# Side steps of the expert scoring stage: their place in VectorE's queue, the order of a wide block's products, and gates for sixteen tokens at a time

## Chip, cores, metric

One core of one Trainium2 chip runs the whole program in one launch. The metric is the device time of the program in microseconds, as the median of several executions.

## What is computed

A two-layer decoder on 256 tokens of width 1024. Layer 0 mixes tokens with a sparse attention, layer 1 with a forgetting attention; each is followed by an expert layer, and at the end stands a norm. The change touches the expert layer alone, which runs once in each layer:

```python
def peer_ffn(x, w_q, sub_keys, u, v):
    q = (x @ w_q).reshape(B, S, PEER_HEADS, 2, hq)
    s_half = jnp.einsum('bshpc,hpkc->bshpk', q, sub_keys)
    top_s, top_i = lax.top_k(s_half, PEER_TOPK)          # 16 of 128, two halves, 8 heads
    cand_s = top_s[..., 0, :, None] + top_s[..., 1, None, :]
    best_s, best_pos = lax.top_k(cand_s.reshape(B, S, PEER_HEADS, 256), PEER_TOPK)
    gate = jax.nn.softmax(best_s, axis=-1)
    h = jax.nn.gelu(jnp.einsum('ted,td->te', u[ec], xc))  # the chosen experts of each token
    return jnp.einsum('te,ted->td', gate * h, v[ec])
```

There are 128 x 128 = 16384 experts. The kernel gathers none: it multiplies every token by all of u, weights the result with a gate that is zero for the experts that were not chosen, and multiplies by all of v.

## The kernel before

All products are of split numbers: a weight tile is rounded (`hi`, a cast on ACT, L116) and the rest is kept beside it (`lo`, a subtraction on VectorE, L117), and hi·hi, hi·lo and lo·hi are added up in PSUM. TensorE is named PE below, VectorE DVE, ScalarE ACT, GpSimd POOL, SyncE SP.

The expert layer (`peer`) has three stages. In the first, x is multiplied by w_q in 16 blocks of columns, and each block is scored against its keys. In the second, **u's stage**, 128 blocks of u (128 experts each) are multiplied with all 256 tokens. In the third, v's stage, 128 blocks of v are multiplied with the gated result. This is about u's stage, whose loop over b stands at L1044 to L1049. One turn of it does this:

- `load_split(uT[b])` (L758): SP loads a tile `raw` of 128x1024, ACT casts it to `hi` (L116), DVE subtracts to get `lo` (L117). Each of `raw`, `hi` and `lo` has three buffers, so that the tiles of block b+3 take those of block b.
- The products, into a PSUM tile `h` of which there are two, so that block b+2 takes that of block b. Even blocks run `feat_block` (L774), called f below: for each of 8 chunks three products of 256 columns (L778, L781, L782). Odd blocks run `wide_block` (L1014), called W: for each chunk one product of 512 columns (hi with both halves of x, L1019) and one of 256 (lo, L1020), alternating. A W block leaves two halves in PSUM, which are added: ACT copies one out (`u`, written to a tile `vraw`, L1022), DVE adds the other (L1023). This is called the add below; it frees the PSUM tile.
- `values(b, o)` (L1025): the gelu on ACT (L1031), and for tokens whose gates stand already a product on DVE (L1035).
- Steps of a generator `aux`, until their nominal costs add up to 1.5 us a block: what is left of the top 16 keys (`top_keys`, L812), the best pairs (`best_pairs`, L905), and the gates (`gate_steps`, L983).

`gate_steps` builds the gates of 8 tokens at a time: DVE compares an index table `iota` with the tokens' two chosen rows (L991, L992), multiplies with the gate's two parts (L994, L995), PE multiplies one-hot by one-hot, 16 products of 128 columns in half precision (L1002, L1003), into PSUM tiles `m`, and the result is multiplied into what stands there by DVE (L1009) or copied by ACT (L1011). The one-hots take a 4 KB buffer of the three called `vhl` and a 2 KB one of the four called `vraw`.

Every engine runs its queue in order. The order is set by a scheduler when the program is built: it takes instructions in the program's order, lets those that it holds ready go ahead, and goes by its own costs. So a step can stand in DVE's queue well before the place at which the loop asked for it, among it before the `lo` and the add of a block that PE is about to need.

```python
        for b in range(NB):
            values(b, (wide_block if b % 2 else feat_block)(load_split(uT[b])))
            if b < 2:
                scores(14 + b, qTs[14 + b])
            while spent < 1.5 * (b + 1):
                spent += next(aux, 1e9)
```

Of the kernel before, what the change touches and what calls it, by code (L numbers as in the profile page):

```python
# [8 lines left out]
F32 = mybir.dt.float32  # L9
F32R = mybir.dt.float32r  # L10
F16 = mybir.dt.float16
# [6 lines left out]
P = 128  # L18
S = 256
# [20 lines left out]
def body(ctx, tc, A, out):  # L40
# [14 lines left out]
    iota = const.tile([P, 4, P, 2], F16, name="iota")  # L55
# [52 lines left out]
    def late_consts():  # L108
        V.tensor_copy(identb, ident)
        GP.iota(iota, pattern=[[0, 4], [1, P], [0, 2]], base=0, channel_multiplier=0, allow_small_or_imprecise_dtypes=True)  # L110
        mtmp = t2k(P)
        SP.dma_start(mtmp, A["cmask"])
        V.tensor_copy(maskb, mtmp)

    def split(raw, hi, lo, eng=None):
        ACT.copy(hi, raw)  # L116
        (eng or V).tensor_tensor(lo, raw, hi.bitcast(F32), ALU.subtract)  # L117
# [639 lines left out]

    def load_split(src, eng=None):  # L758

        raw = tl(ustr, "raw", [8, P], bufs=3)  # L760
        SP.dma_start(raw, src)
        hi = tl(ustr, "hi", [8, P], F32R, 3)
        lo = tl(ustr, "lo", [8, P], F32R, 3)
        if eng is None:
            split(raw, hi, lo)
        parts = []
        for hf in range(2):
            cs = slice(4 * hf, 4 * hf + 4)
            if eng is not None:
                split(raw[:, cs], hi[:, cs], lo[:, cs], eng[hf])  # L770
            parts.append((hi[:, cs], lo[:, cs]))
        return parts
# [12 lines left out]
    def peer(li, norm, mark):  # L785
# [27 lines left out]
        def top_keys():  # L813
            for b in range(16):
                for tt in range(2):
                    s1, s2 = sb[b][:, tt], ar(S2 + ((2 * b + tt) % 4) * 128, P)
                    V.max(topf[:, tt, b, 0:8], s1)
                    V.max_index(idx[:, tt, b, 0:8], topf[:, tt, b, 0:8], s1)
                    V.match_replace(s2, topf[:, tt, b, 0:8], s1, FMIN)
                    V.max(topf[:, tt, b, 8:16], s2)  # L820
                    V.max_index(idx[:, tt, b, 8:16], topf[:, tt, b, 8:16], s2)
                    yield 1.4
# [17 lines left out]
        for b in range(16):  # L840
# [11 lines left out]
            while tops + 1.4 <= min(2.8 * len(scored), 2.5 * (b - 2)):  # L852
                tops += next(keyed)
# [52 lines left out]
        def best_pairs():  # L906
# [22 lines left out]
            for hh in range(16):  # L929
# [7 lines left out]
                yield 1.0  # L937
# [24 lines left out]
            for tt in range(2):  # L962
                yield 2.0
# [19 lines left out]
        def gate_steps():  # L983


            for t0 in range(0, S, 8):
                ohb, ol = t4k(2, 4, P, 2, dt=F16), t2k(4, P, 2, dt=F16)
                o2, oh = ohb[:, 0], ohb[:, 1]
                row = lambda i: (hkT[:, i, t0:t0 + 8].rearrange("p (q t) -> p q t", q=4)
                                 .unsqueeze(2).broadcast_to((P, 4, P, 2)))  # L990
                V.tensor_tensor(o2, iota, row(1), ALU.is_equal)  # L991
                V.tensor_tensor(oh, iota, row(0), ALU.is_equal)  # L992
                yield 1.4
                V.tensor_tensor(ol, oh, row(3), ALU.mult)  # L994
                V.tensor_tensor(oh, oh, row(2), ALU.mult)  # L995
                pgs = []
                for q in range(2):
# [7 lines left out]
                yield 1.4  # L1005
                for q in range(2):
# [6 lines left out]
                yield 1.2  # L1013

        def wide_block(parts):
            o = pst("h")
            for c in range(8):
                hi, lo = parts[c // 4]
                PE.matmul(o, hi[:, c % 4], x2[:, c].rearrange("p a t -> p (a t)"), start=c == 0, stop=False)  # L1019
                PE.matmul(o[:, :S], lo[:, c % 4], xh[:, c], start=False, stop=c == 7)  # L1020
# [23 lines left out]
        for b in range(NB):  # L1044
# [3 lines left out]
            while spent < 1.5 * (b + 1):  # L1048
                spent += next(aux, 1e9)  # L1049
# [161 lines left out]
```

## Time and profile before

| what | value |
|---|---|
| median of 3 runs | 1937.56 us (1936.56 to 1938.04) |
| the profiled execution's own time | 1937.12 us |
| its span, first to last instruction | 1935.4 us |
| mean granted clock of PE | 0.997 |
| busy PE, DVE, ACT, POOL | 1900.9, 1435.3, 1030.1, 107.7 us |
| PE waiting to start, where W blocks wait for the add (L1019 for DVE L1023) | 5.2 us, 7 times |
| the same by the weight load, which comes first | 8.3 us, 14 times |

Matmuls are pipelined: a row's duration is longer than the time until the next one starts, so what PE takes for a piece of work is read from start to start, and not as a sum of durations. The same holds, less strongly, for DVE: the next instruction starts about 0.08 us before the one before it ends.

### The profile page before, as it was taken

Reading aid. Unit: us, or ns where it says so; the run is one execution under the profiler, and the core shown is the slowest. Engines: PE = TensorE matmul, PEld = TensorE weight load, DVE = VectorE, ACT = ScalarE, POOL = GpSimd, SP = SyncE. Lnnn points to the kernel's source line nnn. Section 1 sums busy time; section 2 is a strip of 40 time slices with the busy share of each in tenths; the row PEclk is TensorE's granted clock in tenths of the full one; section 3 lists DMA queues with packets and bytes.
Section 4 is the critical chain, followed back from the end, with each engine's and each line's share of the span. In section 5 each row is a group of like instructions: output and inputs, shape, how many; then the busy total and the mean of one; then the engine's idle time right before and its main releaser. Section 6 shows DMA issues by size and latency. Waiting matters only on the chain.

```text
span 1935.4 us, 32159 instructions
## 1 busy us (share of the span) xinstructions
PE 1900.9 (98%) x12107; PEld 1660.8 (86%) x12107; DVE 1435.3 (74%) x3016; ACT 1030.1 (53%) x2038; POOL 107.7 (6%) x76
## 2 busy tenths in 40 slices
PE   8889999999999999999999999999999999999998
PEld 6767989999999888888889799899999988888886
DVE  8687997788899655565676799968889975555555
ACT  4475655555555544454554655555555554444444
POOL 2001700000000000000000061000000000000001
PEclk9999999999999999999999999999999999999999
DMA  6713445545545665567644245554545556555564
GB/s 228 271 39 121 163 164 177 174 164 164 164 164 164 218 206 195 192 213 256 220 156 152 71 164 162 172 182 161 167 161 164 164 178 215 195 195 192 191 205 141
DMA packets 91051, 340.79 MB, mean 176 GB/s; under 512 B 9968, under 2 KB 12432, under 8 KB 85776
## 3 DMA queue, kind: packets, MB, share of 16 engines
q1 hardware_dynamic: 90608, 338.22, 52.9%
q8 instruction: 95, 1.56, 0.3%
q14 instruction: 60, 0.49, 0.1%
q10 hardware_dynamic: 288, 0.52, 0.1%
HBM read 334.48 MB, written 4.19 MB: 175 GB/s over the span
## 4 chain that ended last, share of the span: by engine, by line
PE 88%; DVE 8%; ACT 3%; DMA 1%; issue 1%; POOL 0%; SPq 0%; ACTq 0%; DVEq 0%
PE m L1071 12%; PE m L1070 12%; PE m L1072 12%; PE h L1019 11%; PE h L778 6%; PE h L781 6%; PE h L782 6%; PE h L1020 6%; DVE lo L117 2%; PE m L203 2%; PE m L201 2%; PE m L202 2%; PE m L1002 2%; PE m L1003 2%; PE m L695 1%; PE m L694 1%
## 5 line engine op out<-in xcount | busy, mean ns | idle before, releaser
L117 DVE TENSOR_TENSOR lo<-raw,hi 128x1024 fp32r<-128x1024 f32 x516 | 633.5, 1228 | 375.5 <-ACT hi L116 373.2
L116 ACT CAST hi<-raw 128x1024 fp32r<-128x1024 f32 (+1 forms) x572 | 576.3, 1010 | 504.2 <-PE m L1072 312.5
L1071 PE MATMUL m<-lo,vhl 128*128 128x512 f32 x1024 | 398.6, 389 | 0.0
L1072 PE MATMUL m<-hi,vhl 128*128 128x512 f32 x1024 | 398.4, 389 | 0.0
L1070 PE MATMUL m<-hi,vhl 128*128 128x512 f32 x1024 | 398.3, 389 | 0.0
L1019 PE MATMUL h<-x,hi 128*128 128x512 f32 x1024 | 372.5, 400 | 5.4 <-DVE vraw L1023 5.2
L1020 PE MATMUL h<-x,lo 128*128 128x256 f32 x1024 | 291.7, 285 | 0.0
L778 PE MATMUL h<-x,hi 128*128 128x256 f32 x1024 | 289.3, 283 | 0.9 <-ACT E L1031 0.9
L782 PE MATMUL h<-x,lo 128*128 128x256 f32 x1024 | 289.8, 283 | 0.0
L781 PE MATMUL h<-x,hi 128*128 128x256 f32 x1024 | 289.7, 283 | 0.0
L1019 PEld LDWEIGHTS h<-x,hi 128*128 128x128 f32 x1024 | 192.4, 188 | 46.5 <-DVE vraw L1023 8.3
L1071 PEld LDWEIGHTS m<-lo,vhl 128*128 128x128 f32 x1024 | 192.2, 188 | 40.3 <-DVE lo L117 0.5
L1070 PEld LDWEIGHTS m<-hi,vhl 128*128 128x128 f32 x1024 | 192.1, 188 | 40.1 <-ACT hi L116 0.4
L1072 PEld LDWEIGHTS m<-hi,vhl 128*128 128x128 f32 x1024 | 192.2, 188 | 39.9
L778 PEld LDWEIGHTS h<-x,hi 128*128 128x128 f32 x1024 | 193.1, 189 | 6.6 <-ACT E L1031 1.4
L782 PEld LDWEIGHTS h<-x,lo 128*128 128x128 f32 x1024 | 192.8, 188 | 0.0
L781 PEld LDWEIGHTS h<-x,hi 128*128 128x128 f32 x1024 | 192.8, 188 | 0.0
L1020 PEld LDWEIGHTS h<-x,lo 128*128 128x128 f32 x1024 | 192.6, 188 | 0.0
L117 POOL TENSOR_TENSOR lo<-raw,hi 128x512 fp32r<-128x512 f32 x56 | 78.8, 1426 | 261.8 <-ACT hi L116 261.6
L117 DVE TENSOR_TENSOR E<-arena,E 128x1024 fp32r<-128x1024 f32 (+2 forms) x60 | 67.1, 1140 | 10.8 <-ACT E L116 10.5
L778 PE MATMUL h<-E,hi 128*128 128x256 f32 x240 | 70.3, 293 | 3.0 <-ACT arena L851 3.0
L116 ACT CAST E<-arena 128x1024 fp32r<-128x1024 f32 (+2 forms) x64 | 58.6, 952 | 21.6 <-PE m L694 9.7
(314 smaller groups left out, 2772.8 us busy)
## 6 DMA issues: line engine op xcount, KB each, us to landing
raw<-in_u SPq DMA_DIRECT2D x256, 512.0 KB, 3.5
raw<-in_v SPq DMA_DIRECT2D x256, 512.0 KB, 4.1
arena<-in_w_in SPq DMA_DIRECT2D x16, 1024.0 KB, 5.9
raw<-in_wq SPq DMA_DIRECT2D x32, 512.0 KB, 3.5
arena<-in_w SPq DMA_DIRECT2D x8, 1024.0 KB, 5.0
arena<-in_w_out SPq DMA_DIRECT2D x8, 1024.0 KB, 5.1
hd<-arena SPq DMA_DIRECT2D x3, 1024.0 KB, 3.9
arena<-hd SPq DMA_DIRECT2D x3, 1024.0 KB, 5.6
```

The source lines that it names most:

```text
L116: ACT.copy(hi, raw)
L117: (eng or V).tensor_tensor(lo, raw, hi.bitcast(F32), ALU.subtract)
L201: PE.matmul(o[:, :n], sh[:, cc, tsl], wh[:, c], start=cc == 0, stop=False)
L202: PE.matmul(o[:, :n], sh[:, cc, tsl], wl[:, c], start=False, stop=False)
L778: t = PE.matmul(o[:, :S], hi[:, c % 4], sh[:, c], start=c == 0, stop=False)
L781: PE.matmul(o[:, :S], hi[:, c % 4], sl[:, c], start=False, stop=False)
L782: PE.matmul(o[:, :S], lo[:, c % 4], sh[:, c], start=False, stop=c == 7)
L1019: PE.matmul(o, hi[:, c % 4], x2[:, c].rearrange("p a t -> p (a t)"), start=c == 0, stop=False)
L1020: PE.matmul(o[:, :S], lo[:, c % 4], xh[:, c], start=False, stop=c == 7)
L1070: PE.matmul(acc[tt][nh], gh[:, ts], vh, start=first, stop=False)
L1071: PE.matmul(acc[tt][nh], gh[:, ts], vl, start=False, stop=False)
L1072: PE.matmul(acc[tt][nh], gl[:, ts], vh, start=False, stop=last)
```

## The change

Five edits, all in `peer` and its helpers.

1. `load_split` keeps the `lo` of the last block that was split, and the loop traces its steps under `issue_after` of it: in DVE's queue each step then stands behind that `lo`. This orders the queue when the program is built; no semaphore is added.
2. The nominal costs change: 1.25 in place of 1.4 for a step of the top keys, 1.3 in place of 1.0 for one of the pairs, 0.4 in place of 2.0 ahead of the transposes, and 1.46 us of steps a block in place of 1.5.
3. A wide block does its eight products of 512 columns first, then its eight of 256.
4. Gates are built for 16 tokens at a time: four operations on 2048 elements in place of eight on 1024, 32 products of PE in one piece in place of two pieces of 16, four PSUM tiles `m` (all there are) for one piece. The one-hots take all three `vhl` buffers.
5. The index table has one copy in place of four (256 elements a partition), and is read by a broadcast.

```diff
     def split(raw, hi, lo, eng=None):
         ACT.copy(hi, raw)
-        (eng or V).tensor_tensor(lo, raw, hi.bitcast(F32), ALU.subtract)
+        return (eng or V).tensor_tensor(lo, raw, hi.bitcast(F32), ALU.subtract)
...
         if eng is None:
-            split(raw, hi, lo)
+            split_of["last"] = split(raw, hi, lo).ins
...
-                    yield 1.4
+                    yield 1.25
...
-            while tops + 1.4 <= min(2.8 * len(scored), 2.5 * (b - 2)):
+            while tops + 1.25 <= min(2.5 * len(scored), 2.5 * (b - 2)):
...
-                yield 1.0
+                yield 1.3
...
-                yield 2.0
+                yield 0.4
...
-            for t0 in range(0, S, 8):
-                ohb, ol = t4k(2, 4, P, 2, dt=F16), t2k(4, P, 2, dt=F16)
-                o2, oh = ohb[:, 0], ohb[:, 1]
-                row = lambda i: (hkT[:, i, t0:t0 + 8].rearrange("p (q t) -> p q t", q=4)
-                                 .unsqueeze(2).broadcast_to((P, 4, P, 2)))
-                V.tensor_tensor(o2, iota, row(1), ALU.is_equal)
-                V.tensor_tensor(oh, iota, row(0), ALU.is_equal)
-                yield 1.4
+            for t0 in range(0, S, 16):
+                o2, oh, ol = (t4k(8, P, 2, dt=F16) for _ in range(3))
+                row = lambda i: (hkT[:, i, t0:t0 + 16].rearrange("p (q t) -> p q t", q=8)
+                                 .unsqueeze(2).broadcast_to((P, 8, P, 2)))
+                index = iota.unsqueeze(1).broadcast_to((P, 8, P, 2))
+                V.tensor_tensor(o2, index, row(1), ALU.is_equal)
+                yield 1.2
+                V.tensor_tensor(oh, index, row(0), ALU.is_equal)
+                yield 1.2
                 V.tensor_tensor(ol, oh, row(3), ALU.mult)
+                yield 1.2
                 V.tensor_tensor(oh, oh, row(2), ALU.mult)
                 pgs = []
-                for q in range(2):
+                for q in range(4):
...
-                yield 1.4
-                for q in range(2):
+                yield 1.2
+                for q in range(4):
...
                     done[1] += 4
-                yield 1.2
+                    yield 0.6
 
         def wide_block(parts):
             o = pst("h")
             for c in range(8):
-                hi, lo = parts[c // 4]
-                PE.matmul(o, hi[:, c % 4], x2[:, c].rearrange("p a t -> p (a t)"), start=c == 0, stop=False)
-                PE.matmul(o[:, :S], lo[:, c % 4], xh[:, c], start=False, stop=c == 7)
+                PE.matmul(o, parts[c // 4][0][:, c % 4], x2[:, c].rearrange("p a t -> p (a t)"), start=c == 0, stop=False)
+            for c in range(8):
+                PE.matmul(o[:, :S], parts[c // 4][1][:, c % 4], xh[:, c], start=False, stop=c == 7)
...
-            while spent < 1.5 * (b + 1):
-                spent += next(aux, 1e9)
+            with tc.issue_after(split_of["last"]):
+                while spent < 1.46 * (b + 1):
+                    spent += next(aux, 1e9)
```

Line numbers move by a few: the add is L1027 after the change (L1023 before), the wide products L1022 and L1024 (L1019, L1020), the gate operations on DVE L993, L995, L997, L999, the gate products L1006, L1007.

How the queues change is shown at three places. The first is DVE's queue early in u's stage of layer 0: `lo_360`, `lo_364` and `lo_369` are the splits of blocks 4, 5 and 6, the tile `vraw_357` is written by the add of block 3, L817 to L821 (L819 to L823 with the change) are steps of the top keys, and L924 and L909 the start of the best pairs. Before:

```order
L117 TENSOR_TENSOR lo_364_2853<-raw_362_2850,hi_363_2852 128x1024
L821 MAX_INDEX arena_58<-arena_58 128x8
L819 MATCH_REPLACE arena_58<-arena_58 128x128
L924 TENSOR_TENSOR arena_58<-arena_58 128x16x8
L820 MAX arena_58<-arena_58 128x8
L924 TENSOR_TENSOR arena_58<-arena_58 128x16x5
L821 MAX_INDEX arena_58<-arena_58 128x8
L924 TENSOR_TENSOR arena_58<-arena_58 128x16x16
L909 CAST arena_58<-arena_58 128x512
L117 TENSOR_TENSOR lo_369_2885<-raw_367_2882,hi_368_2884 128x1024
L1023 TENSOR_TENSOR vraw_357_2804<-h_356_2787,vraw_357_2804 128x256
```

and with the change:

```order
L117 TENSOR_TENSOR lo_360_2831<-raw_358_2828,hi_359_2830 128x1024
L822 MAX arena_58<-arena_58 128x8
L819 MAX arena_58<-arena_58 128x8
L823 MAX_INDEX arena_58<-arena_58 128x8
L820 MAX_INDEX arena_58<-arena_58 128x8
L821 MATCH_REPLACE arena_58<-arena_58 128x128
L117 TENSOR_TENSOR lo_364_2868<-raw_362_2865,hi_363_2867 128x1024
L822 MAX arena_58<-arena_58 128x8
L823 MAX_INDEX arena_58<-arena_58 128x8
L117 TENSOR_TENSOR lo_369_2900<-raw_367_2897,hi_368_2899 128x1024
L1027 TENSOR_TENSOR vraw_357_2819<-h_356_2802,vraw_357_2819 128x256
```

The add of block 3 stands behind the split of block 6 in both. Between the splits of blocks 5 and 6 stood eight operations of steps, and now two; over the whole way from the split of block 3 to this add it is 20 in place of 24, and the four that went are the start of the best pairs, which is now asked for behind the split of block 6. Further on, the sixteen steps of the best pairs (L932 to L936 before) stood between the splits of blocks 7 and 14, two or three a block; now they stand between those of blocks 8 and 22, one a block and at two places two.

The second place is PE's queue where gates are built (the tile `m` is the gates' PSUM, `h` that of a block). Before, a piece of 16 gate products stands inside a block, most often behind the ninth product of a W block:

```order
L1020 MATMUL h_664_4921<-x2_59,lo_663_4918 128x256
L1019 MATMUL h_664_4921<-x2_59,hi_662_4917 128x512
L1002 LDWEIGHTS vhl_644_4816
L1002 MATMUL m_652_4852<-vhl_644_4816 128x128
L1003 LDWEIGHTS vhl_644_4816
L1003 MATMUL m_652_4852<-vraw_645_4817,vhl_644_4816 128x128
```

and with the change a piece of 32 stands between two blocks:

```order
L784 MATMUL h_616_4617<-x2_59,lo_615_4614 128x256
L1022 MATMUL h_621_4653<-x2_59,hi_619_4649 128x512 x8
L1024 MATMUL h_621_4653<-x2_59,lo_620_4650 128x256 x8
L1006 LDWEIGHTS vhl_610_4606
L1006 MATMUL m_624_4678<-vhl_611_4607,vhl_610_4606 128x128
L1007 LDWEIGHTS vhl_610_4606
```

Of a layer's 32 pieces before, 31 stood inside a block; of the 16 now, one does (the first, inside block 39), and the last stands behind block 112 (before: inside block 123). The wide products stand in runs of eight.

The third place is DVE's queue at the same stage, with the change: the four operations of one piece (L993, L995, L997, L999), each behind a split of its own or the next.

```order
L117 TENSOR_TENSOR lo_644_4798<-raw_642_4795,hi_643_4797 128x1024
L1027 TENSOR_TENSOR vraw_622_4670<-h_621_4653,vraw_622_4670 128x256
L993 TENSOR_TENSOR vhl_639_4791<-iota_63,hkT_337_2674 128x2048
L1039 TENSOR_TENSOR E_336_2670<-vraw_623_4674,E_336_2670 128x48
L995 TENSOR_TENSOR vhl_640_4792<-iota_63,hkT_337_2674 128x2048
L117 TENSOR_TENSOR lo_649_4834<-raw_647_4831,hi_648_4833 128x1024
L1039 TENSOR_TENSOR E_336_2670<-vraw_632_4746,E_336_2670 128x48
L1013 SCALAR_TENSOR_TENSOR E_336_2670<-m_624_4678,E_336_2670 128x55x4
L1013 SCALAR_TENSOR_TENSOR E_336_2670<-m_625_4687,E_336_2670 128x55x4
L997 TENSOR_TENSOR vhl_641_4793<-vhl_640_4792,hkT_337_2674 128x2048
L1027 TENSOR_TENSOR vraw_637_4778<-h_636_4761,vraw_637_4778 128x256
L117 TENSOR_TENSOR lo_655_4865<-raw_653_4862,hi_654_4864 128x1024
```

The rows are those of blocks 56 to 58: a split of every block, an add of every second, and one or two long steps between.

On POOL the index table is built ahead of everything else in both; with the change a clearing of 64x1024 (L369) stands between the first two of POOL's four splits of the program's first weights. SP's queue of u's loads stands as it was.

## Rows read from the trace of the kernel before

**Rows 1.** The page, part 1: busy time, share of the span, instructions.

```profile
PE 1900.9 (98%) x12107; PEld 1660.8 (86%) x12107; DVE 1435.3 (74%) x3016; ACT 1030.1 (53%) x2038; POOL 107.7 (6%) x76
```

**Rows 2.** PE's timeline, ends of layer 0's u stage: start, duration, instruction, count.

```profile
239.92 0.37 PE L778 MATMUL h<-x,hi 128*128 128x256 f32 x1
...
643.70 0.40 PE L1070 MATMUL m<-hi,vhl 128*128 128x512 f32 x1
```

**Rows 3.** PE's timeline, first product of an f block and of the next block.

```profile
331.75 0.28 PE L778 MATMUL h<-x,hi 128*128 128x256 f32 x1
...
334.59 0.47 PE L1019 MATMUL h<-x,hi 128*128 128x512 f32 x1
```

**Rows 4.** PE's timeline, first product of a W block and of the next block.

```profile
317.53 0.39 PE L1019 MATMUL h<-x,hi 128*128 128x512 f32 x1
...
320.34 0.28 PE L778 MATMUL h<-x,hi 128*128 128x256 f32 x1
```

**Rows 5.** PE's timeline, a piece of 16 gate products inside a W block.

```profile
430.19 0.39 PE L1019 MATMUL h<-x,hi 128*128 128x512 f32 x1
...
431.29 0.22 PE L1003 MATMUL m<-vraw,vhl 128*128 128x128 f16 x1
...
431.52 0.39 PE L1019 MATMUL h<-x,hi 128*128 128x512 f32 x1
```

**Rows 6.** The waits of the whole span: us in total, times, longest us.

```profile
PEld h L1019 <- DVE vraw L1023: 8.3, 14, 1.1
...
ACT hi L116 <- PE h L1019: 50.7, 37, 2.2
...
PE h L1019 <- DVE vraw L1023: 5.2, 7, 0.9
```

**Rows 7.** Timeline of PE and DVE, a W block (block 5) that waits.

```profile
254.06 0.42 DVE L909 CAST arena<-arena 128x512 f16<-128x512 uint32 x1
...
254.39 1.22 DVE L117 TENSOR_TENSOR lo<-raw,hi 128x1024 fp32r<-128x1024 f32 x1
...
254.96 0.28 PE L782 MATMUL h<-x,lo 128*128 128x256 f32 x1
...
255.53 0.42 DVE L1023 TENSOR_TENSOR vraw<-h,vraw 128x256 f32<-128x256 f32 x1
...
256.00 0.50 PE L1019 MATMUL h<-x,hi 128*128 128x512 f32 x1 [0.77 <-DVE vraw L1023]
```

**Rows 8.** Timeline of ACT, DVE and PE, a W block that starts late.

```profile
367.37 1.05 ACT L116 CAST hi<-raw 128x1024 fp32r<-128x1024 f32 x1 [0.58 <-ACT vraw L1034]
...
368.45 1.23 DVE L117 TENSOR_TENSOR lo<-raw,hi 128x1024 fp32r<-128x1024 f32 x1 [1.47 <-ACT hi L116]
369.59 0.42 DVE L1023 TENSOR_TENSOR vraw<-h,vraw 128x256 f32<-128x256 f32 x1
...
370.09 0.47 PE L1019 MATMUL h<-x,hi 128*128 128x512 f32 x1
370.40 0.28 PE L1020 MATMUL h<-x,lo 128*128 128x256 f32 x1
```

**Rows 9.** PE's timeline in v's stage: first and tenth of ten wide products.

```profile
799.91 0.39 PE L1072 MATMUL m<-hi,vhl 128*128 128x512 f32 x1
...
801.95 0.39 PE L1072 MATMUL m<-hi,vhl 128*128 128x512 f32 x1
```

**Rows 10.** Groups of instructions of DVE: line, operation, shapes, count, busy us, mean ns.

```profile
L991 DVE TENSOR_TENSOR vhl<-iota,hkT 128x1024 f16<-128x1024 f16 x64 | 43.6, 682 | 0.1
...
L897 DVE TENSOR_TENSOR arena<-arena 128x2048 f16<-128x2048 f16 x8 | 9.8, 1222 | 0.1
```

**Rows 11.** A stretch: length, busy PE, PEld, DVE, ACT, POOL, clock, DMA, GB/s.

```profile
540.00:640.00 100.00, 100.00 (x806) 93.54 (x805) 90.95 (x165) 54.85 (x135) 0.00 (x0) 1.00 0.49 160
```

**Rows 12.** POOL's timeline at the program's start.

```profile
7.91 3.49 POOL L117 TENSOR_TENSOR E<-arena,E 128x512 fp32r<-128x512 f32 x2 [1.37 <-ACT E L116]
11.46 1.84 POOL L369 MEMSET lo<- 64x1024 f32 x2
```

More of the change, by code (lines that the diff above doesn't have):

```diff
@@ L54, in body @@
     maskb = const.tile([P, P], F32R, name="maskb")
-    iota = const.tile([P, 4, P, 2], F16, name="iota")
+    iota = const.tile([P, P, 2], F16, name="iota")
     dram = ctx.enter_context(tc.tile_pool(name="dram", bufs=1, space=bass.MemoryType.DRAM))
@@ L109, in late_consts @@
         V.tensor_copy(identb, ident)
-        GP.iota(iota, pattern=[[0, 4], [1, P], [0, 2]], base=0, channel_multiplier=0, allow_small_or_imprecise_dtypes=True)
+        GP.iota(iota, pattern=[[1, P], [0, 2]], base=0, channel_multiplier=0, allow_small_or_imprecise_dtypes=True)
         mtmp = t2k(P)
@@ L756, in fox @@
         return out_proj(HL, A["w_out1"], oh, ol, 3, [marks[i] for i in (2, 5, 7)]), marks[7]
+    split_of = {}
     def load_split(src, eng=None):
```

## The prediction

> **What bounds it now.** I read the page's busy shares first: PE is busy for 98% of the span [rows 1], so a gain must come from time in which PE does less than it could. Its timeline says where that is, because the change moves work in u's stage alone. In layer 0 that stage runs from 239.92 to 643.70, 403.8 us [rows 2]. An undisturbed f block takes 2.84 us from its first product to the next block's [rows 3], a W block 2.81 [rows 4], and a piece of 16 gate products adds 1.33 - 0.35 = 0.98 to the W block that it interrupts (1.33 from the product before it to the next wide one [rows 5]; 0.35 is a pair without a piece, an eighth of 2.81). 64 x 5.65 + 32 x 0.98 = 393.0. Two scores and three small transposes, ten short products, take some 1.5 by my estimate. So about 9.3 us of a layer's stage are lost, near 19 us in both.
>
> Where they go is read from the waits and two places of the timeline. The only engine that PE waits for there in any amount is DVE, for the add that frees a W block's PSUM tile: PE stands idle 5.2 us by the products and 8.3 by the weight loads that precede them, in 14 blocks [rows 6]. One of them is shown in full [rows 7]. PE's last product of block 4 starts at 254.96 and would let the next start 0.12 later, but block 5 starts at 256.00, 0.05 after the add of block 3 has ended; 0.92 is lost. DVE had steps to do up to 254.39 (L909 the last), then the split of block 6, and the add straight behind it, with no idle time between. The second loss hardly shows among the waits [rows 8]. Here DVE was idle, not behind. The cast of the tile three blocks on starts at 367.37, when the last wide product of the W block has released `hi`; the split starts at 368.45, the add behind it at 369.59, and ends at 370.01. PE starts at 370.09, its first product lasts 0.47 and not 0.39 as in [rows 4], and the next comes 0.31 later where 0.23 is usual (0.35 for a pair less 0.12 for its narrow product). So cast, split and add stand in a row that is just as long as the f block between, and W blocks start up to 0.1 late.
>
> **The change, term by term.**
>
> *The steps behind the last split, and their costs.* In DVE's queue the add of block 3 still stands behind the split of block 6, but four operations fewer stand ahead of it. One, L909, takes 0.33 from start to start [rows 7]; the widest L924 reads 256 elements and I count it alike, the two narrow ones half that, together about 1.0. So the 0.92 lost at block 5 goes. Behind that the best pairs stand one a block and not two or three. A pair of blocks leaves DVE 5.65 - 2 x 1.14 - 0.33 = 3.0 us (a split is 1.14 from start to start, [rows 7]), 1.5 a block, which is the pace asked for; so DVE does not fall behind again, and the adds that PE waited for stand 1 us or more early. I take 7.0 us of the two layers' waits; the ends are 5.2 and 8.3 [rows 6].
>
> *Eight wide products first.* The cast waits for the last wide product 37 times [rows 6]. That product now starts 7 x 0.23 = 1.6 us after the block's first and not 2.5, so the cast is done when the block ends, and the split starts at once: the add of rows 8 then ends about 1 us before PE needs it. What is late next is the add behind the long gate operations (1.2 us each, [rows 10]), with roughly 1 us in hand. Rows 8 lose 0.31 - 0.23 = 0.08; at half of that, over the 62 W blocks of a layer that have another two blocks ahead, it is 2.5 a layer. What the stage loses besides the waits, 9.3 - 4 = 5 a layer, bounds the term at 10 from above; it is 0 if the adds stay late. I take 5.0, half of what rows 8 would give at every W block.
>
> *The same edit, in the products themselves.* A pair of a wide and a narrow product takes 2.81/8 = 0.351. In v's stage nine wide products in a row take 2.04, 0.227 each [rows 9]; narrow ones in a row take 2.84/24 = 0.118 [rows 3]. By that a W block takes 2.76, 0.05 less, 6.4 us over 128 W blocks. If the pair's 0.351 is the two products' own cost, it is 0. I take 4.5, nearer to the rows of v's stage, whose wide products have the same shapes and types.
> The Trainium skill (TensorE: Matmul & The Clock Gate, Back-to-back issue gap) gives a product alone a gap of its columns at the clock and 2.5 ns, whatever stands beside it; by that the order of the same 16 products is neutral, this term is 0, and the time is 4.5 us longer. The rows do not bear out its level (0.227 for 512 columns against its 0.216), and its neutrality no row tests with the same operands.
>
> *Gates for sixteen tokens.* The last of the 16 products starts 1.10 after the wide one ahead of the piece [rows 5]; less that one's own 0.23, 15 steps take 0.87, 0.058 each. So 32 in one piece take 0.98 + 16 x 0.058 = 1.91 and not 1.96: 0.05 to 0.07 for each of the 32 pieces that go, 2.0 us. The pieces stood inside f blocks in part, where they may have waited for operands; the ends are 0 and 4. DVE's four operations shorten from 8 x 0.68 to 4 x 1.22 [rows 10], 0.58 a piece, 19 us over both layers. DVE is no bound (91% busy late in the stage, [rows 11]), so I count this at nothing; it keeps the terms above true.
>
> *What is added.* The one-hots take all three `vhl` buffers, so the first operation of a piece waits on DVE until PE has done with the piece before; the pieces stand some five blocks apart, and the next first operation two or three blocks behind the products, so this costs nothing but around the first piece, which stands inside block 39 and whose last operation is queued behind the split of block 40: 0.4 for both layers, between 0 and 1. On POOL a clearing now stands between the first two splits of the program's start. The two took 3.49, and a clearing is half of 1.84 [rows 12]; PE needs the second one for its fourth chunk, so at most 0.9 is lost, but the next weights come from a load that ends later, so I take 0.3. SP's queue of loads is unchanged, its raw tiles are asked for by splits that come no later. ACT gets fewer and longer waits; it is at 55% [rows 11].
>
> **The sum.** 7.0 + 5.0 + 4.5 + 2.0 = 18.5 gained, 0.7 lost: 17.8. The profiled execution's own time is 1937.1 (its span 1935.4 and 1.7 around it), so 1919.3; the median shown lies 0.4 higher, 1919.7. I round it to **1919.5**. Two thirds of it is what the stage loses today, and its weakness is that it leaves only a third of that loss standing.
>
> **The rivals.**
> - *The order of the products is neutral*: 0.351 is what a wide and a narrow product cost wherever they stand, W blocks stay at 2.81, and there is no third term: 1919.5 + 4.5 = 1924. For it: the rows of v's stage have other operands. Against it: ten products in a row keep that pace there [rows 9]. 0.15. The page's rule above would have it so.
> - *The waits only move.* Long gate operations, 1.22 in place of 0.68, stand in front of a split or an add; late starts stay, and half of the 7.0 comes back as waits for other adds. 1919.5 + 5.0 + 3.5 = 1928. For it: DVE is 91% busy. Against it: its work shrinks. 0.13.
> - *Slower: the `vhl` buffers.* With one set of one-hots, DVE's queue stops at a piece's first operation until PE has finished the piece before, and splits and adds behind it come late. In 100 us DVE has 9 to spare [rows 11], 1.4 in the 16 us of five blocks and a piece (5 x 2.82 + 1.91). A stop of 2.1 costs PE 0.7 at each of 32 pieces, 22 us, more than the 17.8: 1942. It decides from stops of 2.0 a piece on (0.6 x 32 = 19); the distance of the pieces speaks against it. 0.05.
> - *The change does little*: the stage stays within 2 us of 403.8, as the losses I put down to the add are PE's own. 1935. The row of idle time in rows 7 speaks against it. 0.05.
>
> **How the numbers follow.** My forecast has 0.62. If all that the stage loses went (18.6 in place of 12.0) and the third term came to 6.4, it would be 1911; from half way to it, 1915, to the first rival it has its own range. That rival and the second reach to 1928, so the range is 1914 to 1929, which leaves out the last two rivals and the ends. A measurement here tells 0.2%, 3.9 us, from no change. Faster by more: 0.62 + 0.15 + 0.13 = 0.90; within it: 0.05; slower: 0.05.
>
> **What would show it.** Right: u's stage of layer 0 near 394.7; the weight load's wait for the add under 1.5 us in all; first products of W blocks at 0.39; W blocks at 2.76 to 2.77; pieces of 32 near 1.9; DVE some 19 us less busy in the gate operations. Wrong: W blocks still at 2.81 (third term), a wait of PE for the gate operations or for `lo`, a wait of DVE's first gate operation for PE of over 1 us at each piece, or a start of the program later by more than 0.9.

## The result, and the profile after

The changed kernel takes 1919.9 us (median of 6 runs, 1918.69 to 1920.65) beside 1937.6 for the kernel before: a ratio of 0.9909, 95% interval 0.9896 to 0.9921, a gain of 17.7 us. The profiled execution took 1920.65 (span 1918.9), 16.5 less than the one of before by their own times.

The page, part 1, answers to [rows 1]. PE loses 8.4 us of busy time (the rest of the 16.5 was idle before), DVE 10.6:

```profile
PE 1892.5 (99%) x12107; PEld 1659.0 (86%) x12107; DVE 1424.7 (74%) x2888; ACT 1036.4 (54%) x2026; POOL 103.3 (5%) x76
```

The ends of u's stage of layer 0 in PE's timeline, beside [rows 2]: 395.18 us in place of 403.78. Layer 1 has the same 395.18, in place of 403.85. So the two stages give 17.3, and the start 0.75 back (the stage begins at 240.67, before at 239.92).

```profile
240.67 0.37 PE L780 MATMUL h<-x,hi 128*128 128x256 f32 x1
...
635.85 0.40 PE L1075 MATMUL m<-hi,vhl 128*128 128x512 f32 x1
```

The longest waits of PE over the whole span, beside [rows 6]. The add (now L1027) is not among them; within the stage (245 to 632) the list of PE's waits is empty.

```profile
PE m L550 <- ACT vhl L555: 3.6, 7, 2.0
PE h L780 <- ACT arena L853: 3.0, 2, 1.5
```

An f block and an undisturbed W block in PE's timeline, beside [rows 3, 4]; a row with x8 stands for eight products. The f block takes 318.27 - 315.42 = 2.85 by the row of its first product (not shown), the W block 321.08 - 318.27 = 2.81, as before:

```profile
318.27 2.03 PE L1022 MATMUL h<-x,hi 128*128 128x512 f32 x8
320.14 1.11 PE L1024 MATMUL h<-x,lo 128*128 128x256 f32 x8
321.08 0.28 PE L780 MATMUL h<-x,hi 128*128 128x256 f32 x1
```

A piece of 32 gate products, beside [rows 5]. From the product before it to the first wide one behind it pass 1.94; less that product's own 0.12 it is 1.82, and the eight wide ones take 2.11 where they take 2.03 above:

```profile
449.44 0.28 PE L784 MATMUL h<-x,lo 128*128 128x256 f32 x1
449.57 0.23 PE L1006 MATMUL m<-vhl,vhl 128*128 128x128 f16 x1
...
451.36 0.22 PE L1007 MATMUL m<-vhl,vhl 128*128 128x128 f16 x1
451.38 2.11 PE L1022 MATMUL h<-x,hi 128*128 128x512 f32 x8
```

And the chain that ended too late in [rows 8], cast, split, add, first wide product, at a W block of after:

```profile
280.76 1.05 ACT L116 CAST hi<-raw 128x1024 fp32r<-128x1024 f32 x1 [0.66 <-PE h L1022]
...
282.38 1.20 DVE L117 TENSOR_TENSOR lo<-raw,hi 128x1024 fp32r<-128x1024 f32 x1
283.51 0.42 DVE L1027 TENSOR_TENSOR vraw<-h,vraw 128x256 f32<-128x256 f32 x1
...
284.31 0.86 PE L1022 MATMUL h<-x,hi 128*128 128x512 f32 x3
```

The add ends at 283.93, 0.38 before the W block starts, though best-pair steps kept DVE busy up to the split. In [rows 8] it ended 0.08 before, with DVE idle. There the cast came behind the last wide product, which starts 2.45 into its block (366.89 - 364.44) and ends at 367.29; here that product starts 1.6 in. The bracket in [rows 8] names an operation of ACT itself, L1034, but that one had ended by 366.79.

The late add of [rows 8] shows in PE's weight loads (PEld), though no wait is listed there. The first two rows are the loads for the undisturbed W block of [rows 4], the last two those for the W block of [rows 8]:

```profile
317.41 0.19 PEld L1019 LDWEIGHTS h<-x,hi 128*128 128x128 f32 x1
317.53 0.19 PEld L1020 LDWEIGHTS h<-x,lo 128*128 128x128 f32 x1
...
370.07 0.19 PEld L1019 LDWEIGHTS h<-x,hi 128*128 128x128 f32 x1
370.18 0.19 PEld L1020 LDWEIGHTS h<-x,lo 128*128 128x128 f32 x1
```

The first load usually stands 0.12 ahead of its product (317.53 in [rows 4]); behind the late add it stands 0.02 ahead (370.09), 0.06 after the add's end. The first product still starts 0.12 after the one before it; it is the second that comes 0.08 late.

### The profile page after: what moved, and what is told of

The parts are those of the page before. It is cut to its first block, busy times and chain, and to the rows that moved or that the text cites. A ratio compares the mean times of both kernels' runs of the same rounds, so it can differ in the third digit from the quotient of the medians.

```text
span 1918.9 us, 32063 instructions
## 1 busy us (share of the span) xinstructions
PE 1892.5 (99%) x12107; PEld 1659.0 (86%) x12107; DVE 1424.7 (74%) x2888; ACT 1036.4 (54%) x2026; POOL 103.3 (5%) x76
## 4 chain that ended last, share of the span: by engine, by line
PE 94%; DVE 2%; ACT 2%; DMA 1%; issue 0%; SPq 0%; ACTq 0%; DVEq 0%
PE h L1022 13%; PE m L1076 12%; PE m L1077 12%; PE m L1075 12%; PE h L780 8%; PE h L783 7%; PE h L784 7%; PE h L1024 6%; PE m L201 2%; PE m L203 2%; PE m L202 2%; PE m L1006 2%; PE m L1007 2%; DMA arena<-in_w_in 1%; PE m L694 1%; PE m L695 1%
## 5 line engine op out<-in xcount | busy, mean ns | idle before, releaser
L784 PE MATMUL h<-x,lo 128*128 128x256 f32 x1024 | 289.0, 282 | 0.0
L1022 PE MATMUL h<-x,hi 128*128 128x512 f32 x1024 | 262.1, 397 | 0.0
L1022 PEld LDWEIGHTS h<-x,hi 128*128 128x128 f32 x1024 | 183.4, 188 | 34.8
L780 PEld LDWEIGHTS h<-x,hi 128*128 128x128 f32 x1024 | 193.1, 189 | 0.0
L784 PEld LDWEIGHTS h<-x,lo 128*128 128x128 f32 x1024 | 193.1, 189 | 0.0
L783 PEld LDWEIGHTS h<-x,hi 128*128 128x128 f32 x1024 | 193.0, 189 | 0.0
L1024 PEld LDWEIGHTS h<-x,lo 128*128 128x128 f32 x1024 | 139.0, 188 | 11.7
L1024 PE MATMUL h<-x,lo 128*128 128x256 f32 x1024 | 142.2, 281 | 0.0
```

The source lines that it names most:

```text
L780: t = PE.matmul(o[:, :S], hi[:, c % 4], sh[:, c], start=c == 0, stop=False)
L783: PE.matmul(o[:, :S], hi[:, c % 4], sl[:, c], start=False, stop=False)
L784: PE.matmul(o[:, :S], lo[:, c % 4], sh[:, c], start=False, stop=c == 7)
L1022: PE.matmul(o, parts[c // 4][0][:, c % 4], x2[:, c].rearrange("p a t -> p (a t)"), start=c == 0, stop=False)
L1024: PE.matmul(o[:, :S], parts[c // 4][1][:, c % 4], xh[:, c], start=False, stop=c == 7)
```

## The experiments

Theory: three parts add up, DVE's queue order (PE's waits for the add), the earlier release of `hi` by the wide products (late starts), and fewer gate pieces; the pace of the products does not change. The rivals were that the row itself is faster, that the new costs do the work and not the queueing, and that one edit alone brings the gain.

The table has one line a kernel; each ratio is to runs of the kernel before on the same chip, and - means not counted. "Stage" is u's stage of layer 0. "Late" counts the W blocks that follow an f block directly and for which the add that frees their PSUM tile ends less than 0.14 us before their first wide product starts. "Wait" is the time by which these first products start after the end of the 0.119 of the product before; "slow first" the time by which the second product stands behind the usual 0.232 after the first. Both are sums over layer 0 from PE's timeline.

| kernel | median us | ratio to before, 95% | stage | late | wait | slow first |
|---|---|---|---|---|---|---|
| before | 1937.6 | 1 | 403.78 | 40 of 62 | 4.0 | 3.0 |
| the change | 1919.9 | 0.9909 (0.9896 to 0.9921) | 395.18 | 2 of 54 | 0.1 | 0.2 |
| a_alternate | 1925.5 | 0.9943 (0.9930 to 0.9957) | 397.90 | 29 of 51 | 1.2 | 2.3 |
| a_no_after | 1927.1 | 0.9945 (0.9932 to 0.9959) | 398.46 | 6 of 54 | 3.0 | 0.7 |
| a_old_costs | 1920.4 | 0.9909 (0.9894 to 0.9924) | 395.19 | - | 0.1 | 0.1 |
| a_gates8 | 1926.2 | 0.9941 (0.9928 to 0.9955) | 397.70 | - | 0.1 | 0.2 |
| a_iota4 | 1919.8 | 0.9910 (0.9897 to 0.9924) | 395.16 | - | - | - |
| b_wide_first | 1933.8 | 0.9982 (0.9973 to 0.9991) | 401.62 | 7 of 62 | 3.1 | 0.6 |
| b_queue | 1930.8 | 0.9968 (0.9955 to 0.9980) | 400.67 | 31 of 62 | 2.1 | 2.6 |
| b_gates16 | 1934.7 | 0.9990 (0.9981 to 0.9999) | 402.54 | - | 4.4 | 2.2 |
| b_rest | 1929.3 | 0.9955 (0.9941 to 0.9969) | 399.66 | 6 of 54 | 3.2 | 0.6 |
| a_half_row | 1924.3 | 0.9929 (0.9915 to 0.9942) | 397.01 | 6 of 53 | 0.8 | 0.5 |
| a_all_wide | 1918.1 | 0.9899 (0.9884 to 0.9914) | 393.19 | - | - | - |
| a_wide_late | 1919.0 | 0.9906 (0.9889 to 0.9922) | 394.22 | - | - | - |

### One part undone: a_alternate

```diff
-                PE.matmul(o, parts[c // 4][0][:, c % 4], x2[:, c].rearrange("p a t -> p (a t)"), start=c == 0, stop=False)
-            for c in range(8):
-                PE.matmul(o[:, :S], parts[c // 4][1][:, c % 4], xh[:, c], start=False, stop=c == 7)
+                hi, lo = parts[c // 4]
+                PE.matmul(o, hi[:, c % 4], x2[:, c].rearrange("p a t -> p (a t)"), start=c == 0, stop=False)
+                PE.matmul(o[:, :S], lo[:, c % 4], xh[:, c], start=False, stop=c == 7)
```

> The changed kernel with the wide block's products alternating again (edit 3 undone); all else as changed. Theory: the pace of the products does not depend on their order, but an order with the wide ones first is done with the tile hi eight products earlier, so the cast and the split of the block three turns later start earlier; so the undisturbed wide block stays at 2.81 to 2.82 us and about 5 us come back as late starts (DVE L117 waiting for ACT L116, L116 waiting for the block's last product): 1925, between 1923 and 1927. Rival A, the wide products in a row run faster (the prediction's third term): the wide block takes 2.85 or more and the time is 1924, without more waits. Rival B, the gain came from the queue and the gates alone: 1920, within 1 us of the changed kernel.

5.6 us came back, 2 x 2.72 by the stages, as the theory said. The undisturbed W block is 2.805 alternating (median of 17) and 2.812 in the row (43): rival A falls, and the row is even 0.007 a block dearer. Timeline of ACT, DVE and PE, one late W block of this kernel, which reads like [rows 8]; the first product lasts 0.47, and the next comes 0.31 behind it:

```profile
356.75 1.05 ACT L116 CAST hi<-raw 128x1024 fp32r<-128x1024 f32 x1 [2.78 <-PE h L1023]
...
357.83 1.23 DVE L117 TENSOR_TENSOR lo<-raw,hi 128x1024 fp32r<-128x1024 f32 x1 [0.92 <-ACT hi L116]
358.97 0.42 DVE L1027 TENSOR_TENSOR vraw<-h,vraw 128x256 f32<-128x256 f32 x1
...
359.47 0.47 PE L1023 MATMUL h<-x,hi 128*128 128x512 f32 x1
359.78 0.28 PE L1024 MATMUL h<-x,lo 128*128 128x256 f32 x1
```

### a_no_after

```diff
-            with tc.issue_after(split_of["last"]):
-                while spent < 1.46 * (b + 1):
-                    spent += next(aux, 1e9)
+            while spent < 1.46 * (b + 1):
+                spent += next(aux, 1e9)
```

> The changed kernel without the queueing of the steps behind the split issued last (the second half of edit 1); the new costs, the wide products in a row and the gates for sixteen tokens stay. Theory: the waits of PE for the add of the wide blocks come back, because steps stand again ahead of the add or of a split in DVE's queue: 2 to 7 us, 1922 to 1927. Rival: the corrected pace of the steps suffices, the add is not late, 1919 to 1921.

7.2 us, just above the theory's upper end; the new costs alone do not suffice. The stage loses 2.98 for first products again, in three blocks for the most part. One in DVE's and PE's timeline (before the first row shown, ten more instructions of the best pairs, L934 to L938, stand behind the split at 264.43):

```profile
266.52 0.20 DVE L934 MAX8 arena<-arena 128x8 f32<-128x50 f32 x1
266.64 1.21 DVE L117 TENSOR_TENSOR lo<-raw,hi 128x1024 fp32r<-128x1024 f32 x1
267.77 0.42 DVE L1027 TENSOR_TENSOR vraw<-h,vraw 128x256 f32<-128x256 f32 x1
...
268.24 0.97 PE L1022 MATMUL h<-x,hi 128*128 128x512 f32 x3 [0.58 <-DVE vraw L1027]
```

### a_old_costs

```diff
-                    yield 1.25
+                    yield 1.4
...
-                yield 1.3
+                yield 1.0
...
-                yield 0.4
+                yield 2.0
...
-                while spent < 1.46 * (b + 1):
+                while spent < 1.5 * (b + 1):
```

> The changed kernel with the old nominal costs of the steps (1.4, 1.0 and 2.0, and 1.5 us of steps a block), still queued behind the split issued last. Theory: the place in the queue is what counts, and the pace little: 1919 to 1922. Rival: the pace is what counts, because steps that are let loose too fast fill DVE for longer than a block takes: 1923 to 1928, and waits of PE for DVE in the part in which the best pairs are taken, where a step was priced 1.0 in place of 1.3.

No difference in time that can be measured; the stage is the same to 0.01 in layer 0 and 0.2 shorter in layer 1. Behind the queueing, edit 2 is worth nothing (the gates' own costs were left new).

### a_gates8

```diff
-            for t0 in range(0, S, 16):
-                o2, oh, ol = (t4k(8, P, 2, dt=F16) for _ in range(3))
+            for t0 in range(0, S, 8):
+                ohb, ol = t4k(2, 4, P, 2, dt=F16), t2k(4, P, 2, dt=F16)
...
-                for q in range(4):
+                for q in range(2):
```

> The changed kernel with the gates built for eight tokens again (edits 4 and 5 undone). Theory: 64 pieces of 16 products at 1.009 in place of 32 pieces of 32 at 1.902, which is 3.7 us: 1923.6, between 1922.5 and 1925.5, the upper end if the shorter steps on DVE make the add late again. Rival: the shift from half precision to the split numbers costs nothing and the pieces differ only by where they stand: 1920, within 1 us.

6.3 us, more than the theory's upper end, but not by late adds. Summed over both layers, 64 pieces cost 66.8 us here, 1.044 each, where 32 cost 60.9, 1.902 each: 5.9 us. An undisturbed piece of 16 would cost 0.98; 26 of the 64 stand inside f blocks, 16 of them start 0.17 late on average and ten 0.10, as here in PE's timeline, where 0.31 pass for a product of 0.12:

```profile
396.17 0.28 PE L783 MATMUL h<-x,hi 128*128 128x256 f32 x1
396.48 0.22 PE L1004 MATMUL m<-vhl 128*128 128x128 f16 x1
```

### a_iota4

```diff
-    iota = const.tile([P, P, 2], F16, name="iota")
+    iota = const.tile([P, 4, P, 2], F16, name="iota")
...
-                index = iota.unsqueeze(1).broadcast_to((P, 8, P, 2))
+                index = iota[:, 0].unsqueeze(1).broadcast_to((P, 8, P, 2))
```

> The changed kernel with the index table built four times over again (1024 elements), of which one copy is read: POOL's queue at the start stands as in the kernel before. Theory 1, the start was later because POOL clears two buffers between its first splits: the stage begins some 0.5 to 0.8 us earlier, and the time is 1919.2. Theory 2, the start was later because the clock granted between 8 and 14 us was 0.50 to 0.83 in that one execution, which is chance: no difference, 1919.9, and a start at full clock or not as it falls.

The medians, 1919.8 and 1919.9, are too coarse to tell 0.6 us; the traces tell more. u's stage begins between 237.6 and 241.2 in the executions profiled, and most of that is the granted clock in the attention of layer 0. The stretch from 95 to 130 us (length, busy PE, PEld, DVE, ACT, POOL, clock, DMA share, GB/s), of the changed kernel, of a_iota4 and of b_gates16, whose stages begin at 240.67, 239.59 and 237.61:

```profile
95.00:130.00 35.00, 31.09 (x185) 23.57 (x183) 25.69 (x89) 21.55 (x82) 0.00 (x0) 0.85 0.13 43
```

```profile
95.00:130.00 35.00, 30.52 (x192) 23.05 (x192) 26.75 (x92) 22.25 (x85) 0.00 (x0) 0.90 0.14 44
```

```profile
95.00:130.00 35.00, 29.85 (x200) 21.18 (x199) 27.68 (x95) 23.45 (x90) 0.00 (x0) 1.00 0.13 41
```

So theory 2 holds in part: the start differs by execution, by up to 3.6 us, though the dip that it named (8 to 14 us: 0.72 in a_iota4 too, 1.00 in the kernel before) is not the one that counts. Among executions with the same clock from 95 to 130 a difference remains. At 0.90 the four with POOL's queue as before (the kernel before, b_wide_first, a_gates8, a_iota4) begin the stage at 239.82 on average, the two with a clearing between the first splits (b_rest, a_half_row) at 240.45; at 0.85 it is 240.07 (b_queue) and 240.69 (four kernels). That would be 0.6 for theory 1, on eleven executions that differ by up to 1.0 within a group. POOL's rows of the changed kernel show where the clearing stands:

```profile
8.25 1.79 POOL L117 TENSOR_TENSOR E<-arena,E 128x512 fp32r<-128x512 f32 x1 [5.92 <-ACT E L116]
10.10 0.95 POOL L369 MEMSET lo<- 64x1024 f32 x1
11.12 1.28 POOL L117 TENSOR_TENSOR E<-arena,E 128x512 fp32r<-128x512 f32 x1
```

But PE's starts behind it speak against theory 1. All fourteen kernels run the same 1595 products in the same order ahead of u's stage. The nine with the clearing start the 31st of them 0.82 later on average than the five without (13.31 and 12.48), but the 61st only 0.12 later (20.38 and 20.26) and the 101st 0.12 (29.68 and 29.56). So the delay is made up by 20 us. The 101st product in PE's timeline, of the kernel before and of the changed one:

```profile
29.88 0.40 PE L202 MATMUL m<-E,x 128*128 128x512 f32 x1
```

```profile
29.98 0.39 PE L202 MATMUL m<-E,x 128*128 128x512 f32 x1
```

Of the 0.75 by which the changed kernel's stage begins later, 0.10 stand there, 0.16 at the 681st product (100 us), and 0.78 at the 761st (119 us): the rest arises in the stretch with the lower clock.

### One part done alone: b_wide_first, b_queue, b_gates16, and the last two edits with the row: b_rest

b_wide_first is the kernel before with the opposite of a_alternate's diff. b_queue is the kernel before with edits 1 and 2:

```diff
...
+            split_of["last"] = split(raw, hi, lo).ins
...
+            with tc.issue_after(split_of["last"]):
+                while spent < 1.46 * (b + 1):
+                    spent += next(aux, 1e9)
```

b_gates16 is the kernel before with the opposite of a_gates8's diff, and b_rest the changed kernel with the diffs of a_no_after and a_old_costs together (at 1.5 us a block).

> The kernel before with edit 3 alone: the wide products of a block in a row, then the narrow ones. Theory: the late starts go, about 5 to 6 us, and the waits for the add stay: 1932, between 1930 and 1934; the undisturbed wide block stays at 2.81. Rival A, the order changes the pace: the wide block falls below 2.78 and 4 us more go. Rival B, the order does nothing while DVE's queue is as before: 1937, within 1 us.

> The kernel before with edits 1 and 2 alone: the steps queued behind the split issued last, at the new costs. Theory: the waits for the add go, 7 to 8 us, the late starts mostly stay: 1930, between 1928 and 1932. Rival: the queueing also removes the late starts, since what made the cast late was DVE's queue and not the tile hi: 1924, between 1922 and 1926; then the order of the products is worth nothing.

> The kernel before with edits 4 and 5 alone: gates for sixteen tokens. Theory: 3.7 us less for PE's pieces, nothing else: 1934, between 1932 and 1936. Rival: the four longer operations stand ahead of the add and the splits and make them later: 1937 to 1940.

> The kernel before with edits 3, 4 and 5 together (wide products in a row, gates for sixteen tokens), without the queueing and with the old costs. Theory: the waits of the first wide products for the add, 3 us a layer with edit 3 alone, stay, the gates give their 1.2 to 1.9 a layer: 1931, between 1929 and 1932.5. Rival: the costs do nothing here either, as they did nothing beside the queueing, and the time is that of the changed kernel without the queueing: 1927, within 1 us.

-3.4, -6.5 and -2.5 us, each inside the theory's bounds, the row 1.8 short of its middle. Together they make 12.4, the change 17.7. The table shows where the rest comes from. The queue alone leaves 31 late blocks, which start at the end of a chain that `hi` holds up; the row alone leaves 7, but in these DVE is behind its steps and PE waits 3.1. Waits and slow firsts fall by 2.4 and 3.4 a layer for one edit each, and by 6.7 for both: 0.9 a layer goes only with the two together. The gates give 1.24 a layer alone and 2.52 behind the other two. By their pieces it would be 0.8 and 2.9: over both layers the kernel before spends 64.6 on them and b_gates16 63.1, as eight of its 32 pieces are broken up by other products, while a_gates8 spends 66.8 and the changed kernel 60.9. The 0.4 by which the stages differ from that, more in the one and less in the other, is not traced. The row alone takes 3.4 a layer from waits and slow firsts but only 2.2 from the stage; its pieces of 16 cost 0.7 a layer more (66.0 in both). b_rest, at 1929.3, is 2.3 slower than a_no_after. Their intervals overlap, but the stages differ by 1.2 in either layer: without the queueing the costs do count a little (0.8 of the 1.2 are at the small transposes, where PE waits for a gelu, below).

### A third order: a_half_row

```diff
...
+            for c in range(4):
+                wide(c)
+            for c in range(4):
+                narrow(c)
+                wide(c + 4)
+            for c in range(4, 8):
+                narrow(c)
```

> The changed kernel with the wide block's products in a third order: four wide ones, then four pairs of a narrow and a wide one, then four narrow ones. The last wide product starts about 2.10 us after the first (7 x 0.232 + 4 x 0.119), between the 1.6 of the row and the 2.5 of the alternating order. Theory (what counts is when the tile hi is free, since cast, split and add follow it): the adds end some 0.48 us later than with the row. With the row 7 of the 54 W blocks counted in layer 0 have an add 0.4 to 0.7 us ahead of them and 2 less than 0.14; alternating it is 29 with less than 0.14, each with a first product that is 0.08 us longer. So about 9 late ones a layer are expected here, 0.4 to 0.7 us, less what the mixed order gains in pace (0.3): a time within 1 us of the changed kernel, and a count of late adds between 2 and 29. Rival (the row itself spares the 0.08 us, whatever the adds do): no late ones, or as many as with alternating products.

The count came out (6 late ones, first products 0.083 longer in these), the time did not: 4.4 us more than the changed kernel, 3.7 by the two profiled executions and all of that in the stages. 0.9 of the 1.8 a layer are the waits and slow firsts of the table. Most of the rest is in the f blocks, whose products step at 0.120 and not 0.1187 for whole blocks on end (2.88 a block and not 2.85). Both paces stand in every kernel with f blocks: of the whole f blocks of layer 0, 41 of 63 step at 0.120 here, 8 of 63 in the changed kernel, 15 of 52 in the kernel before and 4 of 50 in a_gates8. What sets the pace of a block is open; no run here changes it alone.

### Every block wide: a_all_wide, a_wide_late

```diff
-            values(b, (wide_block if b % 2 else feat_block)(load_split(uT[b])))
+            values(b, wide_block(load_split(uT[b])))
```

a_wide_late has `if b % 2 or b > 11` in the first of these lines.

> The changed kernel with every block of u done as a wide block, so that the 128 narrow blocks of both layers go and 128 adds come in. Theory: PE is all that bounds u's stage now, and a narrow block of 2.85 becomes a wide one of 2.82: 3.8 us less, 1916; DVE gets 64 adds of 0.33 a layer, 21 us, and has 50 of 394 idle, so it keeps up. Rival: cast, split and add stand in a row that is longer than the one block between, the adds come late at half of the blocks and more, and each late one costs 0.08 us and up: 1926 to 1935.

> The changed kernel with every block from the twelfth on done as a wide block, while blocks 0 to 11 alternate between narrow and wide as in the changed kernel; in that stretch steps of the top keys keep VectorE nearly full, and with wide blocks throughout PE waited 0.5 us there for an add in each layer. Theory: 116 narrow blocks of 2.85 become wide ones of 2.82, 3.5 us, and the early wait does not come: u's stage at 393.0 to 393.5 in both layers, 1916.5, between 1915 and 1918. Rival: DVE, at up to 98% with wide blocks throughout, is late at other places instead, as it was once in layer 1's stage (0.5 us): 1918 to 1920, no better than the changed kernel.

a_all_wide is the fastest by median, 1918.1, but its interval overlaps that of the changed kernel: no gain in time over it is shown. Its stages are 393.19 and 394.18, 3.0 less in both, where 3.8 would have given 393.3 each. DVE keeps up but for three waits. u's stage, first of the changed kernel, then of a_all_wide (columns as above):

```profile
241.00:635.00 394.00, 394.00 (x3079) 369.75 (x3078) 343.42 (x700) 224.88 (x493) 0.00 (x0) 1.00 0.53 171
```

```profile
241.00:635.00 394.00, 393.47 (x2579) 346.46 (x2578) 362.83 (x760) 246.79 (x557) 0.00 (x0) 1.00 0.54 172
```

DVE goes from 343 to 363 of 394. a_wide_late did not take the early wait out without others: PE waits for the add twice in layer 0's stage, 1.5 us in all, and as much in layer 1's, as its rival said.

## Why the prediction was right, and where a step failed

1919.5 was forecast, 1919.9 came. One of the four terms failed, and the other three were larger than taken; that the sum came out within 0.4 us is luck.

- **Waits for the add (7.0).** The waits of the first wide products fall from 4.02 to 0.13 a layer, 7.8 in both. The mechanism was right, its place only half: I gave all of it to the queue. The queue alone takes 2.0 of the 3.9 a layer; the rest needs `hi` to come free earlier as well. That the new costs matter was wrong: a_old_costs.
- **Late starts (5.0).** The slow firsts fall from 3.0 to 0.2 a layer, 5.6. I took half of 0.08 at each of 62 blocks; it is 0.075 at 40 of them. The mechanism was right, but "W blocks start up to 0.1 late" misread [rows 8]: there the first product starts on time, its weight load stands 0.10 late, and the second product is late.
- **The products themselves (4.5).** This is the step that failed: "nearer to the rows of v's stage, whose wide products have the same shapes and types". The wide products of u's stage keep 0.233 in the row, v's 0.227 [rows 9], and the undisturbed W block goes from 2.807 to 2.812, a loss of 0.6 over both layers in place of a gain of 4.5. The lower end, 0, was the right one, and the rival with 0.15 was right about its mechanism; its time of 1924 did not come because the other terms were larger. The Trainium skill (TensorE: Matmul & The Clock Gate, Back-to-back issue gap) gives the gap from which I worked out a neutral order for a product alone, and says that in a stream of weight loads and products both set the spacing. That the order is neutral was my inference; it holds here to 0.007 of 2.81. The level of that gap, 0.216 for 512 columns, no row shows (0.233 in u's stage).
- **Gates (2.0).** 64 pieces cost 64.6, 32 cost 60.9: 3.7. An undisturbed piece of 16 costs 0.982 and one of 32 1.902, which gives 2.0 for 32 pieces, as worked out; the other 1.7 are the late entries of pieces inside f blocks, which I had named and kept for the end of the range. What these pieces waited for is not shown.
- **Not seen: the gelu.** PE waited once a layer for a PSUM tile that the gelu reads, here in the timelines of ACT and PE of before, behind three small transposes. ACT had loaded its function tables twice by then, 1.28 each, for the exponential of the softmax (L940) and back for the gelu (L1031). The wait is gone in every kernel with the queueing or the new costs, 0.6 a layer; the loads are still there (308.42 and 311.37 in the changed kernel). Which part of the new order takes the wait away, no run shows.

```profile
311.11 1.28 ACT L940 ACT_TABLE_LOAD   x1
312.40 0.42 ACT L940 ACTIVATE arena<-arena 128x256 f32<-128x256 f32 x1
312.84 1.28 ACT L1031 ACT_TABLE_LOAD   x1
314.13 0.38 ACT L1031 ACTIVATE E<-h 128x256 f32<-128x256 f32 x1
```

```profile
313.83 0.27 PE L965 MATMUL g<-cst,arena 128*128 128x128 f32 x1
314.57 0.38 PE L778 MATMUL h<-x,hi 128*128 128x256 f32 x1 [0.47 <-ACT E L1031]
```

- **What is added.** The first piece costs 1.91, as the others do: 0 and not 0.4. The clearing on POOL costs 0.12 on average by 20 us, where 0.3 was taken and 0.9 was the bound; the start that came 0.75 later is for the most part the granted clock of that execution. DVE's gate operations fell from 175.0 us to 155.8, the 19 forecast; the page's busy time fell by 10.6 only, since it counts instructions that overlap once.

Terms as measured: 7.8 + 5.6 - 0.6 + 3.7 + 1.2 = 17.7, beside 17.3 by the stages; 0.75 less at the start leaves the 16.5 of the two profiled executions. The medians differ by 17.7, since executions of one kernel begin the stage at different times (below). The forecast's 17.8 came so near because its misses cancel: 5.1 too much in one term, 3.1 too little in three, 1.2 not seen.

## What to carry to other kernels

Where an engine's queue holds both urgent work (what frees a buffer that the bound engine takes next) and side steps, tie the side steps behind the urgent ones; once they were tied, guessing their costs well did nothing here. Where cast, split and add in a row are as long as the block that covers them, look at what starts the row: reordering products so that an operand's last reader comes earlier was worth 5.6 us behind the other edits (3.4 alone) and cost next to nothing in pace (0.007 a block). Test such edits together: two that shorten one chain at different ends gave more together than the sum of each alone.

## What the runs showed of the hardware

- A first product that starts 0.05 to 0.08 after the end of the add that released it has its successor 0.08 to 0.11 late, although no wait of that first product is listed. The delay stands in the weight load: of the W blocks of layer 0 before, 18 had the add 0.06 to 0.09 ahead, their first load 0.08 to 0.12 late and their second product 0.08 to 0.10 late; with the add 0.14 ahead or more, the second product was on time to 0.01 (20 blocks). In the kernel before that cost 3.0 us a layer, beside 4.0 of late first products.
- A half-precision piece is dear at its end: the first split-number product behind it takes 0.316 to the next and not 0.232 (wide), 0.20 and not 0.12 (narrow), some 0.084 more in the five kernels in which it was read. Since that product itself starts 0.026 after the last gate product, where gate products step at 0.058, a piece costs some 0.06 beyond its products (2 x 0.982 - 1.902); that is what longer pieces save.
- Wide products of the same shape and type step at 0.233 in u's stage and 0.227 in v's; what differs in them is open.
- The granted clock between 95 and 130 us was 0.85, 0.90 or 1.00 on average over the stretch in the executions profiled, and the start of u's stage moved with it, from 237.6 at 1.00 to 241.2 at 0.85. Executions of one kernel differ alike: of 22 of the kernel before, those with a mean clock of 0.998 took 1935.2 to 1935.8 us, those with 0.994 or 0.995 took 1937.2 to 1939.8. What brings a dip was not tried.
